# The first feed-forward reads a copy of x transposed by the host, loads its first operands in small pieces, and alternates between two output blocks

## The chip, the core and the metric

The kernel runs on one core of a Trainium2 chip. The metric is device time in microseconds, taken for the whole program; 2007.43 us is the median of three runs before the change (2007.25 to 2007.64). A difference of about 0.2%, or 4 us, is what a measurement of this kernel can tell from none.

The core has a matrix engine (PE, with its weight load shown as PEld), a vector engine (DVE), a scalar engine (ACT), GpSimd (POOL), and a queue engine (SP) that here issues nearly all transfers between device memory and the on-chip memory. Each engine works through its own list in order; they meet at semaphores.

## The reference

One layer of a hybrid encoder: x is 1024 tokens by 1024 features in float32. What matters here is the first step.

```python
def swiglu_ffn(x, w_gu, w_down):
    gu = x @ w_gu
    g, u = jnp.split(gu, 2, axis=-1)
    return (jax.nn.silu(g) * u) @ w_down

x = layer_norm(ALPHA * x + 0.5 * swiglu_ffn(x, ffn1_w_gu, ffn1_w_down), ln1_g, ln1_b)   # first feed-forward
x = layer_norm(ALPHA * x + hybrid_mixer(x, ...), ln2_g, ln2_b)                          # linear attention, top-k attention
x = layer_norm(ALPHA * x + 0.5 * swiglu_ffn(x, ffn2_w_gu, ffn2_w_down), ln3_g, ln3_b)   # second feed-forward
```

The hidden width is 2816, which is 22 blocks of 128: `w_gu` is 1024 by 5632, its left half for the gate and its right half for the up product. The output has the shape of x.

## The kernel before

**Precision.** Every matrix operand is held as two parts: `split` (L94 to L97) lets ACT round the float32 source to the matrix format (L96, the high part) and then lets DVE subtract that from the source (L97, the low part). A product of two operands is three matmuls: high by high (L336), high by low (L337), low by high (L338).

**Orientation.** The first product needs x with features on the partitions and tokens along the row, while x lies in memory by tokens. So blocks of 128 tokens are loaded by rows into the tiles `xin`, and `turn_in` (L278) has PE transpose four 128 by 128 pieces into a bank `tp` of the accumulator memory (L282), from where `split` makes the two parts. There are two `tp` banks.

**Seven products.** The feed-forwards cut x into four quarters, by feature half and token half. `sums["11"]`, `["21"]`, `["12"]`, `["22"]` are these quarters (first digit the feature half, second the token half), each four slices of 128 features by 512 tokens. From the second group of hidden blocks on, a recombination with seven products instead of eight is used, for which four more operands T1, T2, T3, T4 are formed from sums and differences of the quarters (L1245 to L1248, two on DVE and two on POOL for each of four blocks, in place in the `xin` tiles). Each of the eight operands is turned and split in four blocks: 32 calls of `turn_in` in this stage, 128 transposes.

**The first group.** `gate_up` (L388) computes the first two hidden blocks with the plain eight products. For token half c, for gate then up (i), two banks are taken, and for feature half k and hidden block f the call `product` adds four steps of three matmuls into bank f: 192 matmuls in all, each 128 by 128 by 512. The weights come from `quad_raw` (L292), 512 KB for a feature half, and `plain_weights` (L300) splits 128 by 1024 values at once. Then `quad` begins the second group with the products A11 by 11, A12 by 21, S4 by 22, S1 by T1, S2 by T2, S3 by T3, A22 by T4.

**The order of the work.** Loads are issued on SP's queue in program order: four pieces of x of 256 KB (features 0 to 511 of tokens 0 to 511), 512 KB of gate weights, four more pieces of x, 512 KB of gate weights, 1 MB of up weights, and the four 512 KB blocks of the second token half (L1336 to L1340). The body of the stage is under `in_order`, which chains the matrix engine's instructions in the order written: first the four turns of "11", then the products, with the other turns put between the steps by a list of due steps (`fills`, built by `spread`; `product` counts steps and runs what is due). What is outside a chain, and the order on all other engines, is decided at build time by a planner that simulates the program on a clock of its own and issues what it believes ready.

After the stage come ten more groups with seven products each, the down product of the feed-forward, the mixer, and the second feed-forward, whose front is the same code with `n` = 2 and operands that are made on chip.

## Time and profile before

| what | value |
|---|---|
| median of three runs | 2007.43 us (2007.25 to 2007.64) |
| profiled execution, first to last instruction (span) | 2003.4 us |
| what the median has above that span | 4.0 us |
| PE busy, share of the span | 1951.1 us, 97% |
| PE busy in the first 84 us | 74.8 us |
| DVE, ACT, POOL busy in the first 84 us | 45.1, 34.3, 27.0 us |
| transposes of the first feed-forward (L282), first 84 us | 128 |
| first matmul of a product begins | 11.07 us |

The page states no time of the profiled execution beside its span, so the span is set against the median of the runs. Times in the trace are microseconds from the first instruction; a row of the timeline gives start, duration, engine, line, operation, output and inputs, and in brackets how long the engine had been idle and what ended it. A row of the windows gives for a stretch the busy time of each engine with its number of instructions, then the granted clock of PE, the share of the transfer engines and GB/s. Matmuls overlap in the pipeline: the step from one start to the next tells more than a duration.

### The profile page before, as it was taken

Reading aid. Unit: us, or ns where it says so; the run is one execution under the profiler, and the core shown is the slowest. Engines: PE = TensorE matmul, PEld = TensorE weight load, DVE = VectorE, ACT = ScalarE, POOL = GpSimd, SP = SyncE. Lnnn points to the kernel's source line nnn. Section 1 sums busy time; section 2 is a strip of 40 time slices with the busy share of each in tenths; the row PEclk is TensorE's granted clock in tenths of the full one; section 3 lists DMA queues with packets and bytes.
Section 4 is the critical chain, followed back from the end, with each engine's and each line's share of the span. In section 5 each row is a group of like instructions: output and inputs, shape, how many; then the busy total and the mean of one; then the engine's idle time right before and its main releaser. Section 6 shows DMA issues by size and latency. Waiting matters only on the chain.

```text
span 2003.4 us, 26962 instructions
## 1 busy us (share of the span) xinstructions
PE 1951.1 (97%) x9752; PEld 1601.7 (80%) x9752; DVE 1478.2 (74%) x2330; ACT 824.8 (41%) x1321; POOL 590.6 (29%) x507
## 2 busy tenths in 40 slices
PE   8999999999999999998999899999999999999997
PEld 6888888888888788777777678788888888888886
DVE  5578778775658767999978567575777887866577
ACT  4332332334333444698643346333333232234331
POOL 3245445450001102143434100054444634510011
PEclk9999999999999999998999899999999999999999
DMA  5345444559665423011205651532444454487664
GB/s 178 111 148 179 158 147 163 174 195 312 204 203 195 131 64 110 28 53 39 79 22 163 172 135 38 177 118 83 147 155 147 168 168 139 166 285 262 198 197 150
DMA packets 193301, 298.43 MB, mean 149 GB/s; under 512 B 16384, under 2 KB 100496, under 8 KB 193168
## 3 DMA queue, kind: packets, MB, share of 16 engines
q1 hardware_dynamic: 189264, 291.48, 44.8%
q10 hardware_dynamic: 3264, 3.15, 0.5%
q0 software_dynamic: 640, 2.10, 0.3%
q8 instruction: 76, 1.25, 0.3%
q14 instruction: 57, 0.47, 0.1%
HBM read 205.96 MB, written 90.70 MB: 148 GB/s over the span
## 4 chain that ended last, share of the span: by engine, by line
PE 79%; DVE 10%; DMA 4%; ACT 3%; issue 2%; POOL 2%; SPq 0%; POOLq 0%; DVEq 0%; ACTq 0%
PE pd L508 18%; PE pq L338 13%; PE pq L337 13%; PE pq L336 13%; DVE junk L802 3%; PE pf L672 2%; PE pf L673 2%; PE pf L674 2%; PE pt L689 2%; PE pt L691 2%; PE pv L1158 2%; PE pt L690 2%; PE tpe L1142 2%; PE tp L282 1%; PE lg L1115 1%
## 5 line engine op out<-in xcount | busy, mean ns | idle before, releaser
L97 DVE TENSOR_TENSOR wloq<-rw,whiq 128x512 fp32r<-128x512 f32 (+1 forms) x208 | 214.7, 1035 | 111.1 <-ACT whiq L96 110.2
L97 DVE TENSOR_TENSOR wlod<-rd,whid 128x1024 fp32r<-128x1024 f32 x154 | 186.1, 1219 | 129.3 <-ACT whid L96 127.8
L96 ACT ACTIVATE whid<-rd 128x1024 fp32r<-128x1024 f32 x154 | 161.0, 1059 | 242.8 <-PE pd L508 174.2
L96 ACT ACTIVATE whiq<-rw 128x512 fp32r<-128x512 f32 (+1 forms) x208 | 163.5, 806 | 224.0 <-POOL rw L322 93.4
L508 PE MATMUL pd<-wlod,whid 128*128 128x512 f32 x616 | 239.8, 390 | 0.9 <-DVE wlod L97 0.8
L508 PE MATMUL pd<-whid,wlod 128*128 128x512 f32 x616 | 239.3, 389 | 0.0
L508 PE MATMUL pd<-whid 128*128 128x512 f32 x616 | 235.0, 391 | 0.0
L336 PE MATMUL pq<-b_h,whiq 128*128 128x512 f32 x576 | 229.1, 398 | 2.0 <-ACT b_h L96 2.0
L337 PE MATMUL pq<-b_l,whiq 128*128 128x512 f32 x576 | 225.5, 391 | 1.3 <-DVE b_l L97 1.3
L338 PE MATMUL pq<-b_h,wloq 128*128 128x512 f32 x576 | 225.3, 392 | 0.0
L224 POOL TENSOR_TENSOR rs<-ve,neghalf 128x1 f32<-128x1 f32 x24 | 33.8, 1410 | 539.1 <-DVE ve L242 539.1
L448 ACT ACTIVATE c<-c 128x512 f32<-128x512 f32 x80 | 50.4, 632 | 239.5 <-DVE c L372 147.6
L336 PE MATMUL pq<-xh,whiq 128*128 128x512 f32 x352 | 137.7, 391 | 0.0
L338 PE MATMUL pq<-xh,wloq 128*128 128x512 f32 x352 | 137.0, 389 | 0.0
L337 PE MATMUL pq<-xl,whiq 128*128 128x512 f32 x352 | 136.9, 389 | 0.0
L508 PEld LDWEIGHTS pd<-wlod,whid 128*128 128x128 f32 x616 | 115.6, 188 | 25.8 <-DVE wlod L97 2.1
L508 PEld LDWEIGHTS pd<-whid 128*128 128x128 f32 x616 | 115.5, 188 | 24.6 <-ACT whid L96 1.0
L508 PEld LDWEIGHTS pd<-whid,wlod 128*128 128x128 f32 x616 | 115.6, 188 | 24.0
L689 PE MATMUL pt<-whi,xh 128*128 128x512 f32 x320 | 130.0, 406 | 3.3 <-ACT stage L1490 1.6
L336 PEld LDWEIGHTS pq<-b_h,whiq 128*128 128x128 f32 x576 | 108.9, 189 | 23.9 <-ACT b_h L96 2.7
L337 PEld LDWEIGHTS pq<-b_l,whiq 128*128 128x128 f32 x576 | 108.9, 189 | 23.4 <-DVE b_l L97 2.1
L338 PEld LDWEIGHTS pq<-b_h,wloq 128*128 128x128 f32 x576 | 108.7, 189 | 23.1
(268 smaller groups left out, 4504.8 us busy)
## 6 DMA issues: line engine op xcount, KB each, us to landing
rw<-in_ffn_w_gu_dram SPq DMA_DIRECT2D x88, 512.0 KB, 4.2
rd<-h_dram SPq DMA_DIRECT2D x154, 256.0 KB, 3.5
h_dram<-c SPq DMA_DIRECT2D x148, 256.0 KB, 2.9
rt<-in_ffn_w_down_dram SPq DMA_DIRECT2D x44, 512.0 KB, 3.4
t_dram<-rt SPq DMA_DIRECT2D x44, 512.0 KB, 2.9
rd<-t_dram SPq DMA_DIRECT2D x88, 256.0 KB, 3.9
rd<-in_ffn_w_down_dram SPq DMA_DIRECT2D x66, 256.0 KB, 3.8
raw<-in_w_in_dram SPq DMA_DIRECT2D x20, 512.0 KB, 3.8
```

The source lines that it names most:

```text
L96: self.nc.scalar.activation(hi, src, AF.Copy)
L97: self.nc.vector.tensor_sub(lo, src, hi)
L336: mm(bank, wh[:, k, :], xh[:, k, :], start=(start and k == 0), stop=False)
L337: mm(bank, wh[:, k, :], xl[:, k, :], start=False, stop=False)
L338: mm(bank, wl[:, k, :], xh[:, k, :], start=False, stop=(stop and k == 3))
L448: nc.scalar.activation(t, t, AF.Silu)
L508: nc.tensor.matmul(bank, left, right, start=(i == 0 and n == 0), stop=(i == ng - 1 and n == 2))
L672: nc.tensor.matmul(pt[:m], wh[:, k, :m], xh[:, k, :], start=(k == 0), stop=False)
L673: nc.tensor.matmul(pt[:m], wh[:, k, :m], xl[:, k, :], start=False, stop=False)
L674: nc.tensor.matmul(pt[:m], wl[:, k, :m], xh[:, k, :], start=False, stop=(k == KD - 1))
L689: nc.tensor.matmul(pt, xh[:, k, cols], wh[:, k % 2, :], start=(k == 0), stop=False)
L802: V.tensor_scalar(junk[:, :n], scores[b], thr, None, ALU.is_ge, ALU.add, accum_out=cnt)
```

## The change

- The host hands the kernel a second input `xT`, x transposed (features by tokens); x itself is still an input, read later where the residual needs it. The `xin` tiles of the first feed-forward now hold, for block b = 4c + j and half h, features 128 (4h + j) onwards of token half c.
- Where the first feed-forward called `turn_in`, it now calls `split_in`: the two parts are made straight from the loaded tile, with no transpose and no `tp` bank. The second feed-forward keeps `turn_in`.
- The first half of the gate weights is loaded in four pieces of 128 KB, each behind a 256 KB piece of `xT`, and split in four pieces of 256 columns, alternating with the splits of "11".
- Then come one piece of "21", the second half of the gate weights in one load, the other three pieces of "21", the up weights, and eight pieces of the second token half.
- In the first group, the two banks take turns at every step of three matmuls instead of every four steps; `product` is cut into `step_of` for that.
- Eight matmuls of the identity with itself, whose result nobody reads, stand ahead of everything in PE's chain.

```diff
@@ -282,27 +282,42 @@
             self.nc.tensor.transpose(pt[:, k, :], src[:, k * P : (k + 1) * P], self.ident)
         self.w.split([t[:, :, j * P : (j + 1) * P] for t in self.sums[name]], pt)
+    def split_in(self, src, j, name):
+
+        self.w.split([t[:, j, :] for t in self.sums[name]], src)
+
...
-    def quad_raw(self, w_gu, c0, halves=(0, 1)):
+    def quad_raw(self, w_gu, c0, halves=(0, 1), between=None):
         r = []
         for k in halves:
             t = self.w.raw(self.uid("rw")).rearrange("p (k f) -> p k f", k=4)
+            r.append(t)
+            if between:
+                for j in range(4):
+                    f = k * 4 + j
+                    between(j)
+                    self.nc.sync.dma_start(t[:, j, :], w_gu[f * P : (f + 1) * P, c0 : c0 + 256])
+                continue
             self.nc.sync.dma_start(t, w_gu[k * 512 : (k + 1) * 512, c0 : c0 + 256].rearrange("(k p) f -> p k f", p=P))
-            r.append(t)
         return r
-    def plain_weights(self, r):
+    def plain_weights(self, r, between=None):
         out = {}
         for k, t in enumerate(r, 1):
             hl = [q.rearrange("p (k f) -> p k f", k=4) for q in self.w.pair(self.uid("q"))]
-            self.w.split(hl, t)
+            if between and k == 1:
+                for j in range(4):
+                    self.w.split([q[:, j, :] for q in hl], t[:, j, :])
+                    between(j)
+            else:
+                self.w.split(hl, t)
             for f in range(2):
                 out[f"A{f + 1}{k}"] = [q[:, :, f * P : (f + 1) * P] for q in hl]
         return out
@@ -329,16 +344,20 @@
     def product(self, bank, left, right, start=True, stop=True):
+        for k in range(4):
+            self.step_of(bank, left, right, k, start and k == 0, stop and k == 3)
+
+    def step_of(self, bank, left, right, k, start, stop):
+
         wh, wl = left
         xh, xl = self.sums[right]
         mm = self.nc.tensor.matmul
-        for k in range(4):
-            mm(bank, wh[:, k, :], xh[:, k, :], start=(start and k == 0), stop=False)
-            mm(bank, wh[:, k, :], xl[:, k, :], start=False, stop=False)
-            mm(bank, wl[:, k, :], xh[:, k, :], start=False, stop=(stop and k == 3))
-            self.step += 1
-            while self.fill and self.fill[0][0] <= self.step:
-                self.fill.pop(0)[1]()
+        mm(bank, wh[:, k, :], xh[:, k, :], start=start, stop=False)
+        mm(bank, wh[:, k, :], xl[:, k, :], start=False, stop=False)
+        mm(bank, wl[:, k, :], xh[:, k, :], start=False, stop=stop)
+        self.step += 1
+        while self.fill and self.fill[0][0] <= self.step:
+            self.fill.pop(0)[1]()
     def bank(self, ps):
         pool, tag, n = ((ps, "y", 2), (ps, "z", 2), (self.ps_pj, "pj", 2))[self.turn % 3]
@@ -424,8 +443,10 @@
             for i, a in enumerate(first):
                 banks = [self.bank(ps) for _ in range(2)]
                 for k in "12":
-                    for f in range(2):
-                        self.product(banks[f], a[f"A{f + 1}{k}"], k + c, start=(k == "1"), stop=(k == "2"))
+                    for j in range(4):
+                        for f in range(2):
+                            ends = [(k, j) == ("1", 0), (k, j) == ("2", 3)]
+                            self.step_of(banks[f], a[f"A{f + 1}{k}"], k + c, j, *ends)
                 for f in range(2):
                     if i == 0:
                         t = h[f, c] = self.c_tile(cp, "c")
@@ -1225,16 +1246,13 @@
         firsts, seconds = range(NB // 2), range(NB // 2, NB)
-        def front(n, first, blocks, held, left, ps, early, fed):
+        def front(n, first, t, held, left, ps, early, fed):
 
             V, G = nc.vector, nc.gpsimd
-
-            def t(b, half):
-                return blocks[b][:, half * 512 : half * 512 + 512]
             def turned(j, name):
                 src = {"T1": (j, 0), "T3": (j + 4, 0), "T2": (j + 4, 1), "T4": (j, 1)}
@@ -1250,7 +1268,10 @@
                         held.pop().close()
                         pool = left.enter_context(tc.tile_pool(name=f"t1_{n}", bufs=1, reuse_waits="tile"))
                         self.sums["T1"] = [pool.tile([P, 4, HT], F32R, name=f"t1{p}_{n}") for p in ("h", "l")]
-                    self.turn_in(t(*src[name]), j, name)
+                    if n == 1:
+                        self.split_in(t(*src[name]), j, name)
+                    else:
+                        self.turn_in(t(*src[name]), j, name)
                     if (j, name) == (3, "T4"):
                         held.pop().close()
                         cp.append((left.enter_context(tc.tile_pool(name=f"prod{n}", bufs=1, reuse_waits="tile")), 8))
@@ -1329,20 +1350,31 @@
                 self.two_sums(half_pair(xp, f"b{names[0]}_"), *names)
             held, xin = two_pools("xin")
             w_gu = a["ffn1_w_gu"][0]
-            raw = []
-            for c in range(2):
-                for b in firsts:
-                    cs = slice(c * 512, (c + 1) * 512)
-                    nc.sync.dma_start(xin[b][:, cs], x[0, b * P : (b + 1) * P, cs])
-                raw += self.quad_raw(w_gu, 0, (c,))
+
+            def t(b, half):
+                return xin[b][:, half * 512 : half * 512 + 512]
+
+            def load(c, j, half):
+                k = 4 * half + j
+                nc.sync.dma_start(t(4 * c + j, half), a["xT"][k * P : (k + 1) * P, c * 512 : (c + 1) * 512])
+
+            raw = self.quad_raw(w_gu, 0, (0,), lambda j: load(0, j, 0))
+            load(0, 0, 1)
+            raw += self.quad_raw(w_gu, 0, (1,))
+            for j in range(1, 4):
+                load(0, j, 1)
             raw = [raw, self.quad_raw(w_gu, FF)]
-            for b in seconds:
-                nc.sync.dma_start(xin[b], x[0, b * P : (b + 1) * P, :])
+            for half in range(2):
+                for j in range(4):
+                    load(1, j, half)
             with self.in_order():
-                for b in firsts:
-                    self.turn_in(xin[b][:, 0:512], b, "11")
-                first = [self.plain_weights(r) for r in raw]
-                work = front(1, first, xin, held, st, ps_ff, [(j, "21") for j in range(4)], ())
+                warm = self.ps_tp.tile([P, P], F32, tag="tp", name="warm")
+                for _ in range(8):
+                    nc.tensor.matmul(warm, self.ident, self.ident, start=True, stop=True)
+                self.split_in(t(0, 0), 0, "11")
+                first = [self.plain_weights(raw[0], lambda j: j < 3 and self.split_in(t(j + 1, 0), j + 1, "11"))]
+                first.append(self.plain_weights(raw[1]))
+                work = front(1, first, t, held, st, ps_ff, [(j, "21") for j in range(4)], ())
             for _ in work:
                 pass
         xp_stack = ExitStack()
@@ -1652,7 +1684,7 @@
             ln_stack.close()
             self.two_sums(self.new_half(0), "T2", "T3")
             first.append(self.plain_weights(raw[1]))
-            work = front(2, first, acc, held, st, ps_ff, (), (4, 5))
+            work = front(2, first, lambda b, half: acc[b][:, half * 512 : half * 512 + 512], held, st, ps_ff, (), (4, 5))
             ordered.close()
             for _ in work:
                 pass
@@ -1716,6 +1748,8 @@
         aps[name] = nc.dram_tensor(
             f"in_{name}_dram", arr.shape, mybir.dt.from_np(arr.dtype), kind="ExternalInput"
         ).ap()
+    arrays["in_xT_dram"] = np.ascontiguousarray(np.asarray(inputs["x"])[0].T)
+    aps["xT"] = nc.dram_tensor("in_xT_dram", (D, T), F32, kind="ExternalInput").ap()
     aps["out"] = nc.dram_tensor("out_0_dram", (1, T, D), F32, kind="ExternalOutput").ap()
     with tile.TileContext(nc, schedule_with_timeline_sim=True) as tc:
         emit(tc, aps)
```

## The prediction

> **What bounds the kernel now.** The first view is the page: the busy time of the engines and the chain of waits that ended last.
>
> ```profile
> span 2003.4 us, 26962 instructions
> PE 1951.1 (97%) x9752; PEld 1601.7 (80%) x9752; DVE 1478.2 (74%) x2330; ACT 824.8 (41%) x1321; POOL 590.6 (29%) x507
> ...
> PE 79%; DVE 10%; DMA 4%; ACT 3%; issue 2%; POOL 2%; SPq 0%; POOLq 0%; DVEq 0%; ACTq 0%
> ```
>
> PE bounds the program, but the shares are an average, and the change touches the first stage alone. So the second view is the windows: the stretch up to the last transpose of that stage, what follows it, and the mixer.
>
> ```profile
> 0.00:84.00 84.00, 74.80 (x368) 60.50 (x369) 45.06 (x69) 34.34 (x52) 27.03 (x29) 1.00 0.43 147
> ...
> 72.00:200.00 128.00, 128.00 (x574) 105.98 (x573) 96.28 (x107) 38.97 (x60) 60.25 (x40) 1.00 0.46 156
> 200.00:400.00 200.00, 200.00 (x884) 165.61 (x883) 157.29 (x171) 64.45 (x98) 91.58 (x60) 1.00 0.48 161
> 400.00:600.00 200.00, 199.94 (x881) 165.00 (x880) 129.35 (x141) 76.12 (x83) 26.42 (x22) 1.00 0.70 227
> ...
> 800.00:1000.00 200.00, 190.21 (x1008) 152.25 (x1006) 189.76 (x564) 159.35 (x296) 71.43 (x86) 0.97 0.18 51
> 1000.00:1200.00 200.00, 186.23 (x1274) 148.21 (x1274) 134.29 (x323) 86.23 (x209) 48.73 (x58) 0.97 0.46 122
> 1200.00:1400.00 200.00, 194.43 (x1295) 161.09 (x1295) 131.84 (x228) 85.76 (x136) 50.86 (x32) 0.99 0.30 101
> ```
>
> From 72 to 600 us PE is never free for want of data (527.94 of 528 us), and DVE has a fifth to spare. So what PE is spared before 84 us is handed on whole: everything behind starts earlier by that much. Idle PE time, 9.2 us, lies in the first 84 us. The third view is the timeline of the start.
>
> ```profile
> 0.74 1.81 SPq L1336 DMA_DIRECT2D xin<-in_x_dram  x4
> 3.91 1.94 PE L282 MATMUL tp<-ident,xin 128*128 128x128 f32 x8 [3.91 <-DMA xin<-in_x_dram]
> 5.07 1.28 ACT L96 ACT_TABLE_LOAD   x1 [5.07 <-PE tp L282]
> ...
> 8.99 1.06 ACT L96 ACTIVATE whiq<-rw 128x1024 fp32r<-128x1024 f32 x1 [1.54 <-DMA rw<-in_ffn_w_gu_dram]
> ...
> 11.07 0.80 PE L336 MATMUL pq<-b_h,whiq 128*128 128x512 f32 x1 [1.36 <-ACT b_h L96]
> ...
> 12.56 0.79 PE L337 MATMUL pq<-b_l,whiq 128*128 128x512 f32 x1 [0.69 <-DVE b_l L97]
> 13.15 0.63 PE L338 MATMUL pq<-b_h,wloq 128*128 128x512 f32 x1
> 13.57 0.63 PE L336 MATMUL pq<-b_h,whiq 128*128 128x512 f32 x1
> 13.71 1.06 ACT L96 ACTIVATE whiq<-rw 128x1024 fp32r<-128x1024 f32 x1 [2.69 <-DMA rw<-in_ffn_w_gu_dram]
> ...
> 15.21 1.06 ACT L96 ACTIVATE whiq<-rw 128x1024 fp32r<-128x1024 f32 x1 [0.45 <-DMA rw<-in_ffn_w_gu_dram]
> 16.37 0.40 PE L338 MATMUL pq<-b_h,wloq 128*128 128x512 f32 x1
> ...
> 23.52 0.50 PE L337 MATMUL pq<-b_l,whiq 128*128 128x512 f32 x1 [0.56 <-DVE b_l L97]
> ```
>
> The first x piece lands at 3.9 us, two blocks are turned, ACT loads its table, the weights land at 8.99 as one 512 KB load, and the first product starts at 11.07. Matmuls then start 0.42 us apart (13.15 to 13.57) and from about 16 us at the full pace. PE last waits at 23.52. The fourth view is the end of the stage on PE.
>
> ```profile
> 83.11 0.39 PE L338 MATMUL pq<-b_h,wloq 128*128 128x512 f32 x1
> 83.34 0.60 PE L282 MATMUL tp<-ident,xin 128*128 128x128 f32 x4
> 83.69 0.48 PE L338 MATMUL pq<-t1h,wloq 128*128 128x512 f32 x1
> 84.01 0.40 PE L336 MATMUL pq<-bT_h,whiq 128*128 128x512 f32 x1
> ...
> 89.27 0.39 PE L338 MATMUL pq<-bT_h,wloq 128*128 128x512 f32 x1
> ```
>
> The full pace is 0.2287 us: 23 steps from 84.01 to 89.27. Four transposes cost 84.01 - 83.11 - 2 x 0.2287 = 0.44 us. At 83.69 the last turn is over.
>
> ```profile
> L282 PE MATMUL tp<-ident,xin 128*128 128x128 f32 x128 | 21.2, 296 | 5.9 <-DMA xin<-in_x_dram 3.9 <-DVE b_l L97 1.9
> ...
> L96 ACT ACTIVATE whiq<-rw 128x1024 fp32r<-128x1024 f32 x8 | 8.5, 1058 | 8.6 <-DMA rw<-in_ffn_w_gu_dram 4.7 <-PE pq L337 3.9
> L96 ACT ACTIVATE whiq<-rw 128x512 fp32r<-128x512 f32 x9 | 5.4, 627 | 10.3 <-PE pq L337 4.8 <-issue 3.7 <-DMA rw<-in_ffn_w_gu_dram 1.8
> L1247 DVE TENSOR_TENSOR xin<-xin,xin 128x512 f32<-128x512 f32 x4 | 4.5, 1136 | 5.0 <-POOL xin L1246 5.0
> ```
>
> Of the 368 PE instructions up to 84 us, 128 are transposes and 240 are matmuls of products, one of them begun at 83.69. So 239 matmuls stood before that point, 239 x 0.2287 = 54.7 us at full pace; the other 29.0 us are the late start, the slow pace, waits, and transposes (24 turns at full pace alone are 24 x 0.44 = 10.6 us).
>
> **The change part by part.** I rebuild the time at which those 239 matmuls are done.
>
> *Start.* The first piece of `xT` has the size of the first piece of x and the same place in the queue, so it lands at 3.9. ACT's table load, which waited for PE's transpose, now waits for the load: 5.2. The high part of 128 by 512 from on-chip memory takes 0.63 (the row above with 512 columns): 5.8. A weight piece of 256 columns is not in the trace; from 0.63 at 512 and 1.06 at 1024 columns it is an estimated 0.41: 6.2, with a hand-over of 0.2 the first matmul starts at 6.4. Bounds: 5.1, if the table is loaded before the data; 10.0, if the pieces land no sooner than the 512 KB did (8.99 plus the two ACT steps).
>
> *Arrival.* The four pairs are 1.5 MB, as many bytes as stood in the queue up to and with the first weights, which landed at 8.99. So the fourth pair lands at about 9.0 and those between at 5.6 and 7.3; the second half of the gate weights (2.25 MB) at about 11.4, between 8.99 and 13.71; all of "21" (3.0 MB) at 13.7, and the up weights as before, from 15.2. PE comes to the fourth slice at 6.4 + 18 x 0.2287 + 1.9 (next item) = 12.4, the split of it is ready two splits of ACT and two of DVE behind 9.0, about 11. To the second half it comes at 13.8, and that is split on ACT (1.06) and DVE (about as long) by 13.7. The up weights are wanted at 19.3 and split by 17.5. So two blocks in turn, with six matmuls for each slice, just hide the loads. With eight loads at 0.45 us each (four took 1.81) SP has issued the four pairs by 4.4, ahead of their landing; 23 issues in place of 16 delay only the next weights, which wait for buffers anyway.
>
> *Slow pace.* In the trace the pace doubles some 3.4 us after PE works without gaps (12.56 to about 16). The granted clock is 1.00 in the row to 84 us, so that column doesn't show it; the starts do. Eight identity matmuls, at the pace of the eight transposes (1.94 us), end near 4, and a gap to 6.4 follows. I take it that they change nothing: from 6.4 to about 10.4 some 10 matmuls at 0.42, each 0.19 too long, cost 1.9 us. Bounds 0 (they suffice) and 3.6 (a stretch twice as long). The Trainium skill, "TensorE: Matmul & The Clock Gate", Part 1, says that the clock is released after about 3.4 us of sustained work, watched in free-running windows. This agrees with the 3.4 us here and gives the same sum; by the full effect of a warm-up it would be 1.9 us less.
>
> *Transposes.* All 128 go from PE: nothing replaces them there, and 54.7 us of matmuls stay. 6.4 + 1.9 + 54.7 = 63.0, against 83.7: 20.7 us earlier. The eight waste matmuls lie in time in which PE has no data.
>
> *Splits.* ACT gains 0.03 us a piece, no matter at 34 of 84 us. DVE's subtraction now has both inputs in on-chip memory, where it had one in the accumulators. What that costs is in this view of the same stage, DVE and POOL rows by time.
>
> ```profile
> 28.00 1.30 POOL L319 TENSOR_TENSOR rw<-rw,rw 128x512 f32<-128x512 f32 x1 [1.23 <-DVE wloq L97]
> 28.45 1.40 DVE L1247 TENSOR_TENSOR xin<-xin,xin 128x512 f32<-128x512 f32 x1
> 29.77 1.33 DVE L97 TENSOR_TENSOR b_l<-tp,b_h 128x512 fp32r<-128x512 f32 x2
> 29.93 1.30 POOL L1248 TENSOR_TENSOR xin<-xin,xin 128x512 f32<-128x512 f32 x1 [0.63 <-DVE xin L1247]
> ...
> 33.67 1.30 POOL L321 TENSOR_TENSOR rw<-rw,rw 128x512 f32<-128x512 f32 x1
> 33.76 1.76 DVE L1247 TENSOR_TENSOR xin<-xin,xin 128x512 f32<-128x512 f32 x1 [2.65 <-POOL xin L1246]
> ...
> 39.41 0.69 DVE L1247 TENSOR_TENSOR xin<-xin,xin 128x512 f32<-128x512 f32 x1 [1.15 <-POOL xin L1246]
> ```
>
> L1247, both inputs in on-chip memory, takes 0.69 us alone and 1.40 or 1.76 beside a POOL operation; the split from `tp` at 29.77 ran two in 1.33 beside one, undisturbed. So up to 32 subtractions (28 ahead of S1 by T1) now can be held up. The Trainium skill, "SBUF — State Buffer", Who interferes with whom, has it as a rule: a DVE instruction with two inputs in SBUF contends with GpSimd reads, one with a single such input doesn't. This trace agrees, and the rule speaks against this change.
>
> The price: POOL works 27.0 us in the stretch to 84 us. If every us of it held DVE up, less the 1.8 that the four L1247 already lose (4 x (1.136 - 0.69)), DVE would need 45.1 + 25.2 = 70.3 us, and has 63.0 - 6.4 = 56.6 us from PE's start to the same point: 13.7 us of stall at worst. With half of it, 57.7 us, DVE just about keeps pace. I take 2 us, nearer the lower end since POOL works in a third of the stretch only, and since three products stand ahead of the first that needs a T operand; bounds 0 and 13.7. If DVE falls behind there, the low part of T1 is late next, and PE waits for it.
>
> *Alternating banks* changes neither number nor shape of matmuls. Both blocks now end three matmuls apart, so two evictions of 0.6 to 0.7 us come together; six banks take turns, and the next product has its own. Nothing; at worst one eviction, 0.7 us, at the four ends.
>
> *Sum.* 20.7 - 2 = 18.7 us. Span 2003.4 - 18.7 = 1984.7; with the 4.0 us by which the median of the runs stands above the span, 1988.7, so **1989 us**. From the bounds: 20.7 + 1.9 + 1.3 = 23.9 earlier at best (1983.5); 20.7 - 3.6 + 1.9 - 13.7 = 5.3 at worst with a timely start (2002.1); that both worst cases meet I leave out of the range.
>
> **The rivals.**
>
> *The pieces land together.* If transfers in flight share the bandwidth, the first pair is complete only when the fourth is. For it: the first x piece landed when 512 KB had been issued behind it. Against: it did land at 3.9, 5 us ahead of the weights. The start is then 10.0, 3.6 us later, and the time 1992.
>
> *DVE becomes the bound of the stage.* Three quarters of the worst stall, 10 us, 8 more than I took: 1997. For it: 1.40 and 1.76 against 0.69. Against: POOL is busy for a third of the stretch only. The rule of the Trainium skill on "SBUF — State Buffer", Who interferes with whom, is the ground for it.
>
> *The transposes were hidden.* If the loads or the splits set the pace throughout, removing PE work brings the start alone, 4.7 us: 2002.7. Against it stands PE without a gap from 24 us on.
>
> *Slower: the planner orders the mixer anew.* The order there comes from a simulated clock, and the start moves on it. From 800 to 1400 us PE idles 9.8 + 13.8 + 5.6 = 29.1 us, with DVE at 95% in the first third, so an order that delays DVE is paid at once. Were that idle time doubled, the program would lose 29.1 - 18.7 = 10.4 us: 2018. It decides from 18.7 us of new idle time. Against it: a start that is earlier by a constant leaves the order of what comes later as it is.
>
> **How the numbers follow.** The forecast has 0.60 (with its own range 1985 to 1993), pieces together 0.13, DVE 0.15, transposes hidden 0.04, the planner's order 0.08, half of it slower and half a part of the gain lost. From 1983 to 1999 it holds the first three, less the tails of the forecast: eight in ten. Faster by over 0.2% (4 us, about what a measurement of this kernel can tell) is all but 0.04 for no change and 0.04 for slower: 0.92.
>
> **What would show it.** No L282 row before 84 us; the first L336 with `b_h` near 6.4; a pace of 0.42 to about 10; PE without a wait from there; T2's first product (84.01 now) near 65; L97 on `b_l` above 0.68 mean, with rows near 1.3 beside POOL; the same PE idle time from 780 to 1380. I am wrong if PE waits for DVE for several us between 25 and 65, if the first product starts past 9, or if the idle time of the mixer moves by more than 5 us.

## The result, and the profile after

The median of four runs of the changed kernel is 1989.86 us (1987.2 to 1991.97), that of four runs of the kernel before 2007.54 us (2007.25 to 2007.8). The ratio is 0.9913, with a 95% interval of 0.9902 to 0.9925: 17.7 us faster, where 18.7 us was forecast. The profiled execution of the changed kernel took 1987.2 us, 1.8 more than its span. These are the busy times and the chain of its page.

```profile
span 1985.4 us, 26743 instructions
PE 1933.6 (97%) x9640; PEld 1589.3 (80%) x9640; DVE 1486.2 (75%) x2333; ACT 824.3 (42%) x1324; POOL 598.8 (30%) x507
...
PE 71%; DVE 12%; DMA 6%; POOL 4%; issue 3%; ACT 3%; SPq 0%; POOLq 0%; DVEq 0%; ACTq 0%
```

PE has 17.5 us less to do (128 transposes, 21.2 us, less 3.8 for the identity matmuls) and still bounds the program, but its part of the chain fell from 79% to 71%, and POOL has doubled its own to 4%. The timeline shows the start, on PE and ACT, and the place where the first product of T2 begins.

```profile
0.73 1.28 ACT L96 ACT_TABLE_LOAD   x1 [0.73 <-PEq L1743]
1.74 3.78 PE L1373 MATMUL warm<-ident 128*128 128x128 f32 x16 [1.74 <-POOL ident masks.py:199]
4.05 0.42 ACT L96 ACTIVATE whiq<-rw 128x256 fp32r<-128x256 f32 x1 [2.03 <-DMA rw<-in_ffn_w_gu_dram]
5.17 0.76 PE L355 MATMUL pq<-b_h,whiq 128*128 128x512 f32 x1
...
6.10 0.39 PE L357 MATMUL pq<-b_h,wloq 128*128 128x512 f32 x1
6.33 0.40 PE L355 MATMUL pq<-b_h,whiq 128*128 128x512 f32 x1
...
12.48 0.50 PE L355 MATMUL pq<-b_h,whiq 128*128 128x512 f32 x1 [0.97 <-ACT whiq L96]
13.74 0.50 PE L357 MATMUL pq<-b_h,wloq 128*128 128x512 f32 x1 [0.53 <-DVE wloq L97]
...
62.16 0.39 PE L357 MATMUL pq<-t1h,wloq 128*128 128x512 f32 x1
62.38 0.39 PE L355 MATMUL pq<-bT_h,whiq 128*128 128x512 f32 x1
```

No transpose stands ahead of 62.38, and the first product of T2 starts there, 21.6 us ahead of the 84.01 before. PE starts its products at 5.17 and is at the full pace from 6.10 (the next start is 0.23 later). It waits twice, 1.5 us in all, for the second half of the gate weights. Its second wait is for DVE's low part of these weights; otherwise it does not wait for DVE on the way. The next rows, of POOL, ACT, DVE and PE, show where it does.

```profile
68.28 1.30 POOL L337 TENSOR_TENSOR rw<-rw,rw 128x512 f32<-128x512 f32 x1
69.61 1.06 ACT L96 ACTIVATE whiq<-rw 128x1024 fp32r<-128x1024 f32 x1 [2.67 <-POOL rw L337]
70.70 1.23 DVE L97 TENSOR_TENSOR wloq<-rw,whiq 128x1024 fp32r<-128x1024 f32 x1 [4.43 <-ACT whiq L96]
76.81 0.68 DVE L404 TENSOR_TENSOR c<-c,pq 128x512 f32<-128x512 f32 x1
77.54 0.50 PE L355 MATMUL pq<-b_h,whiq 128*128 128x512 f32 x1 [1.40 <-DVE c L404]
```

POOL ends its sums of the gate weights (L334 to L337) at 69.6, four of some 1.5 us in a row. ACT and DVE, which had waited 2.67 and 4.43 us, split them, and the additions of products queued behind these splits on DVE, up to L404, end at 77.5. PE needs the bank that L404 empties and loses 1.40 us. The groups of instructions up to 84 us show one reason why POOL is late; the fence behind it has a row of the same view of the kernel before.

```profile
L97 DVE TENSOR_TENSOR b_l<-xin,b_h 128x512 fp32r<-128x512 f32 x20 | 16.4, 850 | 1.9 <-ACT b_h L96 1.8
L97 DVE TENSOR_TENSOR bT_l<-xin,bT_h 128x512 fp32r<-128x512 f32 x8 | 10.7, 1364 | 0.0
...
L1266 POOL TENSOR_TENSOR xin<-xin,xin 128x512 f32<-128x512 f32 x4 | 6.7, 1672 | 5.5 <-DVE xin L1265 5.5
```

```profile
L1248 POOL TENSOR_TENSOR xin<-xin,xin 128x512 f32<-128x512 f32 x4 | 5.2, 1295 | 2.9 <-DVE xin L1247 2.9
```

DVE's subtraction with two inputs in on-chip memory takes 0.85 and 1.36 us in the mean, against 0.69 undisturbed; POOL's operation takes 1.67 in place of 1.30. Both engines pay. Behind this stage some of the gain is given back. The windows of after from the first down matmul, from the first of the mixer and from the first score product on, and those of before at the same points:

```profile
434.00:650.10 216.10, 214.16 (x958) 176.46 (x957) 146.81 (x175) 84.87 (x89) 9.26 (x5) 1.00 0.69 224
650.10:1089.60 439.50, 421.74 (x2274) 344.35 (x2273) 363.75 (x872) 262.48 (x499) 138.07 (x190) 0.98 0.24 73
1089.60:1985.40 895.80, 868.30 (x4525) 713.72 (x4523) 630.78 (x902) 325.86 (x507) 246.88 (x165) 0.99 0.50 161
```

```profile
454.00:668.80 214.80, 213.99 (x957) 176.32 (x956) 146.05 (x174) 84.96 (x89) 9.26 (x5) 1.00 0.70 225
668.80:1106.90 438.10, 421.91 (x2273) 343.28 (x2272) 365.12 (x872) 262.30 (x499) 134.98 (x190) 0.98 0.24 73
1106.90:2003.40 896.50, 870.37 (x4525) 715.29 (x4523) 629.77 (x902) 326.39 (x507) 246.21 (x165) 0.99 0.50 161
```

Of the 20.0 us that are left at the first down matmul (454.0 to 434.0), 1.3 go in the down product (216.1 us for 214.8) and 1.4 in the mixer (439.5 for 438.1); 0.7 come back after it (895.8 for 896.5). What the down product lost shows in its own rows, of ACT and PE, and in the row of SP at which the loads behind those of x (L1314, before L1293) are issued; first after, then before.

```profile
449.49 0.33 SPq L228 DMA_DIRECT2D g_bc<-in_ln_g_dram  x1
...
461.37 1.06 ACT L96 ACTIVATE whid<-rd 128x1024 fp32r<-128x1024 f32 x1 [15.23 <-DMA rd<-h_dram]
462.48 1.20 PE L529 MATMUL pd<-whid 128*128 128x512 f32 x4 [1.12 <-ACT whid L96]
```

```profile
468.36 0.33 SPq L228 DMA_DIRECT2D g_bc<-in_ln_g_dram  x1
...
481.22 0.97 PE L508 MATMUL pd<-whid 128*128 128x512 f32 x3
```

PE waits 1.12 us for a piece of h that is still being loaded; before it did not wait there (its row has no bracket). PE came 20.0 us earlier, but SP issued the load of L228, which stands ahead of the next pieces, only 18.9 us earlier: 15.5 us behind the first down matmul, where it was 14.4.

### The profile page after: what moved, and what is told of

Same layout as the page of the kernel before. It is cut to its first block, busy times and chain, and to the rows that moved or that the text cites. A ratio compares the mean times of both kernels' runs of the same rounds, so it can differ in the third digit from the quotient of the medians.

```text
span 1985.4 us, 26743 instructions
## 1 busy us (share of the span) xinstructions
PE 1933.6 (97%) x9640; PEld 1589.3 (80%) x9640; DVE 1486.2 (75%) x2333; ACT 824.3 (42%) x1324; POOL 598.8 (30%) x507
## 3 DMA queue, kind: packets, MB, share of 16 engines
q8 instruction: 76, 1.25, 0.3%
## 4 chain that ended last, share of the span: by engine, by line
PE 71%; DVE 12%; DMA 6%; POOL 4%; issue 3%; ACT 3%; SPq 0%; POOLq 0%; DVEq 0%; ACTq 0%
PE pd L529 18%; PE pq L355 10%; PE pq L356 10%; PE pq L357 10%; DVE junk L823 3%; PE pf L693 3%; PE pf L694 3%; PE pf L695 3%; PE pt L710 2%; PE pv L1179 2%; PE pt L712 2%; PE pt L711 2%; PE tpe L1163 2%; DMA t_dram<-rt 1%; DMA rd<-in_ffn_w_down_dram 1%
## 5 line engine op out<-in xcount | busy, mean ns | idle before, releaser
L97 DVE TENSOR_TENSOR wloq<-rw,whiq 128x512 fp32r<-128x512 f32 (+2 forms) x211 | 212.7, 1010 | 122.5 <-ACT whiq L96 121.3
L96 ACT ACTIVATE whiq<-rw 128x512 fp32r<-128x512 f32 (+2 forms) x211 | 164.2, 797 | 213.2 <-POOL rw L337 105.6
```

Of the source, the lines that this page charges most:

```text
L96: self.nc.scalar.activation(hi, src, AF.Copy)
L97: self.nc.vector.tensor_sub(lo, src, hi)
```

## Experiments

The theory: the gain is the removed transposes (some 16 us) and a start some 5 us earlier through the small pieces, handed on whole until PE waits for something that did not come earlier by as much. The rivals: the start alone makes the gain, because loads or splits set the pace; the identity matmuls or the alternation carry a part; what is lost behind 77 us is not POOL's lateness but the spread from run to run. The kernels below ran on three chips, the kernel before on each of them, so ratios are compared, and times on one chip. Line numbers are those of the changed kernel; in the two kernels named pieces2 they are one higher.

**The changed kernel again (after_again).** Nothing is edited.

> The changed kernel once more, to see where its runs differ (1987.2 to 1992.0 us, while the kernel before stayed within 0.6 us). Theory A, the spread arises at the start, where the matrix engine's pace may or may not have doubled by the first product: then a slower execution shows first matmuls 0.42 us apart and S2 by T2 begins later than 62.4 us, by up to 1.6 us. Theory B, the spread arises in the mixer, where the granted clock dips to 0.97: then S2 by T2 begins at 62.4 us again in every profile, and what differs lies behind 640 us. Time: 1990 us, within 2.5 us.

Measured: 1992.3 us, ratio 0.9929 (0.9916 to 0.9941). The first 84 us repeat: full pace from the start, T2's first product at 63.0, waits of 1.6 and 0.5 us for the second half of the weights and of 1.5 for L404. The down product waits 1.9 us in place of 1.1. With the third measurement below, the gain in the medians is 17.7, 13.5 and 14.5 us, and single traces differ behind 430 us.

**Without the identity matmuls (no_warm).**

```diff
-                warm = self.ps_tp.tile([P, P], F32, tag="tp", name="warm")
-                for _ in range(8):
-                    nc.tensor.matmul(warm, self.ident, self.ident, start=True, stop=True)
```

> The eight identity matmuls are left out, all else as in the changed kernel. Theory A, they double the pace before the first product: without them the first 8 matmuls from 5.2 us start 0.42 us apart, 1.6 us in all, and the stage ends 1.6 us later (S2 by T2 at 64.0, 1991.5 us). Theory B, the slow pace is hidden behind the second half of the gate weights, for which PE waits anyway (1.0 us to 12.48 and 0.5 us to 13.74): then the slow pace is seen, but S2 by T2 comes at most 0.5 us later and the time stays within noise. As the prediction took it, the eight are without effect: then the pace at 5.2 us is the full one here too.

Measured: 1993.05 us, ratio 0.9939 (0.9927 to 0.9952), not told apart from the changed kernel. Its timeline on PE:

```profile
5.07 0.79 PE L355 MATMUL pq<-b_h,whiq 128*128 128x512 f32 x1 [5.07 <-ACT b_h L96]
...
10.23 0.56 PE L357 MATMUL pq<-b_h,wloq 128*128 128x512 f32 x1
10.63 0.40 PE L355 MATMUL pq<-b_h,whiq 128*128 128x512 f32 x1
...
80.22 0.79 PE L355 MATMUL pq<-b_h,whiq 128*128 128x512 f32 x1 [3.33 <-DVE c L404]
```

Products start some 0.4 us apart until 10.63, so the identity matmuls do what the prediction denied them: they bring the full pace forward, in three traces by 3 to 5 us. It is worth next to nothing here. With half the pace PE comes later to the second half of the gate weights and waits for it 0.3 us in place of 2.1; T2's first product stands at 63.0 in both traces. The longer wait for L404 (3.33 against 1.5) was seen in one trace of this kernel, whose execution was the slowest of its five (1998.19 us), and whether the edit causes it stays open. With it the first down matmul comes at 439.2, 4.5 us later than in after_again; PE then does not wait for h in the down product, and 2.5 us of the 4.5 are left at the first mixer matmul (654.1 against 651.6).

**The old order of blocks (no_turns).**

```diff
-                    for j in range(4):
-                        for f in range(2):
-                            ends = [(k, j) == ("1", 0), (k, j) == ("2", 3)]
-                            self.step_of(banks[f], a[f"A{f + 1}{k}"], k + c, j, *ends)
+                    for f in range(2):
+                        self.product(banks[f], a[f"A{f + 1}{k}"], k + c, start=(k == "1"), stop=(k == "2"))
```

> The two output blocks one after the other, four steps each, as before the change; loads in pieces, xT and identity matmuls stay. Theory A: alternation hides the arrival of the slices; without it PE needs the fourth slice after 9 matmuls, at 7.3 us, while it is split near 9.9, so PE waits some 2.5 us there. Of this 1.5 us are won back, since PE comes later to the second half of the weights and need not wait for it: net 0.5 to 1 us. Theory B: taking banks in turn has a price or a gain of its own on PE; then the step between matmuls (0.2287 us) changes and the time moves by more than 2 us.

Measured: 1992.65 us, ratio 0.993 (0.9917 to 0.9944); T2's first product at 62.8. PE waits 0.3 us more at 8.05 and less later. Two blocks in turn are worth nothing that can be measured, with the pieces landing as they do.

**The old loads (big_loads).** The pieces of `xT` and the gate weights are loaded in the order and size of before, and split whole; the rest of the change stays.

```diff
-            raw = self.quad_raw(w_gu, 0, (0,), lambda j: load(0, j, 0))
...
+            for half in range(2):
+                for j in range(4):
+                    load(0, j, half)
+                raw += self.quad_raw(w_gu, 0, (half,))
...
-                self.split_in(t(0, 0), 0, "11")
-                first = [self.plain_weights(raw[0], lambda j: j < 3 and self.split_in(t(j + 1, 0), j + 1, "11"))]
-                first.append(self.plain_weights(raw[1]))
+                for j in range(4):
+                    self.split_in(t(j, 0), j, "11")
+                first = [self.plain_weights(r) for r in raw]
```

> xT, alternation and identity matmuls stay; the loads go back to their old order and size: four pieces of xT, 512 KB of gate weights as one load split at once, four pieces, 512 KB. Theory A: the start sets the time, so the first product begins near 10 us and its low weights come near 11.3, and the stage ends 4 to 4.5 us later (S2 by T2 near 66.5, about 1994 us). Theory B: DVE, busy 8 of every 8 us from 16 to 64 us, paces the stage or POOL paces what follows (PE waits 1.4 us at 77.5): then most of the late start is given back by 100 us and the loss is 1 to 3 us.

Measured: 1996.35 us, ratio 0.9952 (0.9939 to 0.9964), 4.05 us above after_again beside it. From its view of the waits on PE up to 445 us:

```profile
PE pq L355 <- ACT whiq L96: 5.5, 1, 5.5
```

The first product starts at 11.04 and T2's at 68.0, 5.0 us later than in after_again. The wait for L404 is gone, since POOL has those 5 us more; the first down matmul is only 3.2 us later. So the pieces bring 5 us at the start, and about a third of it is paid back at L404.

**The transposed copy alone (xT_only).** Old loads, old order of blocks, no identity matmuls: the three edits above together. Of the change, only `xT` in place of the transposes is left, with its second token half still in eight pieces.

> The kernel before with the transposed copy alone: no transposes, but the old order and size of the loads, the blocks one after the other, and no identity matmuls. Theory A, the transposes were PE work on the path that sets the end: 24 turns at full pace are worth 10.6 us and the first eight, at the slow pace, up to 4 us more; the first product begins near 10.1 to 11 us, at the slow pace for 3.4 us, and S2 by T2 near 67 to 69 us (84.0 before), so about 1994 to 1997 us. Theory B, the transposes were hidden behind the loads and the splits: then S2 by T2 comes no sooner than 79 us and the time is above 2001 us.

Measured: 1996.45 us against 2006.55 of the kernel before on that chip, ratio 0.9951 (0.9937 to 0.9964).

```profile
10.32 0.79 PE L355 MATMUL pq<-b_h,whiq 128*128 128x512 f32 x1 [10.32 <-ACT whiq L96]
```

The start has moved by 0.7 us (11.07 to 10.32), and T2's first product is at 67.48, 16.9 us ahead of before_again's 84.35. The transposes were on the path: the rival by which they were hidden falls. In time 10.1 us of these 16.9 are left; in the two profiled traces the lead is still 16.9 us at the first down matmul and 11.8 at the end.

**POOL's sums of x on DVE (dve_sums).** In the first feed-forward the sums of L1264 and L1266 go to DVE; so POOL has less to do and DVE is disturbed less.

```diff
-                        G.tensor_sub(t(j + 4, 0), t(j + 4, 1), t(j + 4, 0))
+                        (V if n == 1 else G).tensor_sub(t(j + 4, 0), t(j + 4, 1), t(j + 4, 0))
...
-                        G.tensor_sub(t(j, 1), t(j, 1), t(j + 4, 1))
+                        (V if n == 1 else G).tensor_sub(t(j, 1), t(j, 1), t(j + 4, 1))
```

> The changed kernel with the eight sums that POOL made for T2 and T4 (13.4 us on POOL there) put on DVE. Theory A, the two engines hold each other up: DVE gets 8 times 0.68 us more, and loses what POOL cost it (b_l 0.85, bT_l 1.36, the two other sums 0.96 and 1.23 us mean, all 0.68 to 0.69 alone: about 12 us), so DVE is less busy to 64 us (57.6 us now, near 51), POOL's weight sums start sooner and PE's wait of 1.4 to 1.5 us for the combined product (L404) goes; about 1.5 us less up to the first down product (434.0 to 434.8 us now). Theory B, DVE's work is what fills these 48 us: then DVE stays busy throughout, T1 comes later, and PE waits for DVE before 64 us.

Measured: 1989.41 us, ratio 0.9919 (0.9904 to 0.9934). The groups up to 84 us, and POOL's last sum of the first weights with DVE's L404 in its timeline:

```profile
L97 DVE TENSOR_TENSOR b_l<-xin,b_h 128x512 fp32r<-128x512 f32 x20 | 13.2, 690 | 2.6 <-ACT b_h L96 2.5
L97 DVE TENSOR_TENSOR bT_l<-xin,bT_h 128x512 fp32r<-128x512 f32 x8 | 7.1, 890 | 0.0
```

```profile
63.98 1.29 POOL L337 TENSOR_TENSOR rw<-rw,rw 128x512 f32<-128x512 f32 x1
...
72.51 0.68 DVE L404 TENSOR_TENSOR c<-c,pq 128x512 f32<-128x512 f32 x1
```

DVE did eight operations more and was busy for less: 55.84 us up to 64 us in place of 57.55. The splits fell from 850 to 690 ns and from 1364 to 890. POOL's sum comes 4.3 us earlier (68.28 to 63.98), L404 too (76.81 to 72.51), and PE's wait for it is gone. That the wait is gone proves little by itself, since PE is later here too (T2's first product at 64.7). But in all eleven traces of kernels with `xT`, L404 begins 8.51 to 8.54 us behind the start of POOL's last sum, wherever PE stands, and in pieces2_dve below, where PE is earlier than in any other (T2's first product at 60.4), L404 begins at 72.05 and PE does not wait. That shows POOL's lateness as the cause of the wait. How much of the lateness comes from longer operations and how much from POOL's own work is not shown, since the edit takes the eight operations off POOL altogether. In this trace a new loss of about that size stands at 13 to 19 us (below), so that the first down matmul gains nothing (434.7).

**The second half of the gate weights in pieces (pieces2), and with the sums on DVE (pieces2_dve, pieces2_dve_b).** The load of the second half is cut into four, each behind its piece of "21", and split in four pieces, as those of the first are; the other two kernels, which are equal, have the edit of dve_sums too.

```diff
-            if between and k == 1:
+            if between:
...
-                    between(j)
+                    if k == 1:
+                        between(j)
...
-            load(0, 0, 1)
-            raw += self.quad_raw(w_gu, 0, (1,))
-            for j in range(1, 4):
-                load(0, j, 1)
+            raw += self.quad_raw(w_gu, 0, (1,), lambda j: load(0, j, 1))
```

> The changed kernel with the second half of the gate weights in four pieces, POOL's sums left on POOL. Theory A: the waits for that half go (1.5 us) and with them the slow window that may follow, so S2 by T2 begins near 61 us; but POOL and DVE still hold each other up, so PE's wait for the combined product (L404) stays and grows by what was won, to about 3 us: the first down product near 434 us, no gain in the time. Theory B: the wait at L404 has nothing to do with POOL's sums: then it goes here too and the first down product comes near 431 us.

> As dve_sums, and the second half of the gate weights too is loaded and split in four pieces, each behind its piece of 21. Theory A: PE's waits for that half (1.0 to 1.6 us for the high part, 0.5 us for the low part) go too, so S2 by T2 begins near 61 us and the first down product near 431.5 us; about 3 us less than the changed kernel. Theory B: the pieces are three issues more and smaller loads, so they land later or ACT's order holds the fifth slice up: then PE still waits 1 us or more between 11 and 14 us.

> The kernel with pieces in the second half and the sums on DVE once more, beside the changed kernel on one chip. Theory A: 3.5 to 4.5 us less up to the first down product (430.3 against 434.0 to 434.8 us), all of which reaches the end: about 4 us less than after_third in the median. Theory B: the mixer takes it back, since its order and the dips of the clock there move: less than 2 us.

Measured: pieces2 1993.16 us, ratio 0.9931 (0.9919 to 0.9943); pieces2_dve 1988.39, ratio 0.9911 (0.9897 to 0.9925); pieces2_dve_b 1986.77, ratio 0.99 (0.9887 to 0.9913). From the waits on PE up to 445 us of pieces2, then of pieces2_dve_b:

```profile
PE pq L356 <- DVE c L405: 3.3, 1, 3.3
...
PE pq L358 <- DVE wloq L97: 0.3, 1, 0.3
```

```profile
PE pq L356 <- ACT whiq L96: 0.4, 1, 0.4
```

The pieces alone take the wait for the weights from 1.5 to 0.3 us and bring T2 to 61.3, and it all goes again in the wait for `c`, 3.3 us. With the sums on DVE that wait is gone, and the first down matmul comes at 430.3 and 431.5. Neither edit by itself brings PE there sooner than the 434.0 to 436.6 of the changed kernel; together they bring 2.5 to 6.3 us. pieces2_dve_b ran 6.1 us below the changed kernel beside it (1992.89); the intervals of the two ratios overlap from 0.9911 to 0.9913. It is the fastest version found. From chip to chip the gain in time is less clear: the ratio of pieces2_dve, 0.9911, is that of the changed kernel's first measurement, 0.9913.

**Again, both kernels (before_again, after_third, before_third).** Nothing is edited.

> The kernel before once more, for a second trace of it. If the spread of the runs comes from where the granted clock dips in the mixer (Theory B of the first look), this trace agrees with the first one to 0.3 us up to the first matmul of the mixer (668.8 us) and may differ by up to 4 us behind it, at the first score product (1106.9 us). If it comes from the start (Theory A), S2 by T2 begins elsewhere than at 84.0 us. Time 2004 to 2008 us.

> The changed kernel a third time, on the same chip as the next three. Theory A: to the first down product it is within 1 us of 434.0 and 434.8 us, unless the wait for the second half of the gate weights near 12 to 14 us lets the clock fall back (seen once in dve_sums, 15.5 to 18.9 us at 0.42 us a matmul), which costs 1.6 us more. Behind 650 us the mixer takes 439 to 443 us to its first score product. Theory B, the mixer's length is the chip's: then it is the same in after_third and before_third of this call. Time 1987 to 1993 us.

> The kernel before a third time, for a third trace: from the first mixer matmul (668.6 to 668.8 us) to the first score product 438.1 and 440.6 us so far, against 439.5 and 443.1 us in the two traces of the changed kernel. Theory A, the planner's new order of the mixer costs about 2 us: 438 to 441 us here, 440 us or more in after_third. Theory B, both draw from one spread: the two overlap fully.

Measured: before_again 2006.67 us, ratio 1.0 (0.9991 to 1.0009); before_third 2007.49, ratio 0.9999 (0.9989 to 1.0009); after_third 1992.89, ratio 0.9925 (0.9911 to 0.994). The traces give the lead of after over before at each point, in us, the second pair from two chips:

| point | after and before | after_again and before_again | after_third and before_third |
|---|---|---|---|
| first product of T2 | 21.6 | 21.4 | 21.2 |
| first down matmul | 20.0 | 19.5 | 17.0 |
| first mixer matmul | 18.7 | 17.0 | 11.7 |
| first score product | 17.3 | 14.5 | 8.8 |
| last down matmul | 18.0 | 14.1 | 9.3 |

The lead at T2 repeats within 0.5 us. What is given back behind it differs, from 3.7 to 11.9 us in single traces. The PE timeline of after_third has its two largest pieces:

```profile
78.56 0.50 PE L355 MATMUL pq<-b_h,whiq 128*128 128x512 f32 x1 [2.28 <-DVE c L404]
...
79.16 0.63 PE L357 MATMUL pq<-b_h,wloq 128*128 128x512 f32 x1
79.58 0.63 PE L355 MATMUL pq<-b_h,whiq 128*128 128x512 f32 x1
...
82.54 0.39 PE L356 MATMUL pq<-b_l,whiq 128*128 128x512 f32 x1
...
467.59 1.58 PE L529 MATMUL pd<-whid 128*128 128x512 f32 x4 [3.61 <-ACT whid L96]
```

The wait at L404 is 2.28 us here, the one in the down product 3.61, and behind the first the pace is 0.42 us until 82.5, which costs some 1.6 us more (8 steps by 0.2). The wait in the down product goes with SP: where L228 is issued 14.0 to 14.4 us behind the first down matmul (before, before_third) there is none; at 15.5 (after) it is 1.1, at 16.1 to 16.6 (no_turns, after_again, after_third) 1.9 to 3.6. The other traces fit in: none at 13.6 and 14.3 (before_again, no_warm), 0.4 to 1.3 us from 14.8 to 15.8 (pieces2_dve, xT_only, dve_sums), 1.8 to 2.2 from 16.4 to 16.7 (big_loads, pieces2_dve_b, pieces2). Why SP comes to its loads later, measured from PE, was not tried.

## Why the prediction was right, and which steps were not

*The matmul term and the transposes held.* 239 matmuls at 0.2287 us are 54.7; from 5.17 that is 59.8, with the two waits of 1.5 us 61.3, and the 240th stands at 62.16, the rest being slower steps at the start and right behind each wait. xT_only shows the transposes on the path: 16.9 us by themselves.

*The number is in part luck.* The forecast had 18.7 us at T2 and all of it at the end. Measured were 21.6 us at T2, since the start and the pace were better than said, and 18.0 at the end of the trace (17.7 in the median), since 3.7 were given back on the way. The two errors nearly cancel here; in the two later measurements, with 13.5 and 14.5 us in the median, they cancel less.

*Start: 5.17 in place of 6.4.* The table load did not wait for the data. It stood at 0.73, which was the case of the stated lower bound; in big_loads and xT_only it did wait for the first piece of `xT` (3.71 and 3.67), as the forecast took it. The pieces landed one after the other: the high part of the first weights is begun at 4.05.

*Slow pace: mis-sized, 0.5 in place of 1.9.* Only the first two steps are slow, 0.59 and 0.34 us; in after_third the first five are, and cost 1.2. The identity matmuls took 3.78 us, not 1.94: 16 rows for 8 instructions, so that PE worked without a gap until the products began. "I take it that they change nothing" was wrong of the pace (no_warm: half of it until 10.63) and right of the time, for another reason: what the pace gains is waited out at the second half of the weights.

*Arrival: the step "that is split on ACT (1.06) and DVE by 13.7" held, "just hide the loads" did not.* PE came to these weights at 11.5 rather than 13.8, since it started earlier and at full pace, and waited 1.5 us. Start and pace, 1.2 and 1.4 us better than said, paid for this.

*Splits: near in size, wrong in place.* From the windows of after:

```profile
0.00:64.00 64.00, 60.77 (x264) 49.71 (x265) 57.55 (x76) 33.07 (x54) 27.92 (x26) 1.00 0.49 165
```

DVE was busy for 57.55 us up to 64, and the forecast had 57.7 if half of POOL's time held it up. That they agree so closely is chance: 5.2 us of the 57.55 are L430 to L432, work that stood behind 84 us in the kernel before. And the low part of T1 was not late for it, as the prediction had it: PE waits for none of DVE's splits of x. The prediction let only DVE pay; POOL paid too (1.30 to 1.67 us), its weight sums came late for the earlier PE, and the price fell due at L404, 1.4 us (1.5 and 2.28 in the others) for the 2 us taken. The Trainium skill, "SBUF — State Buffer", Who interferes with whom, says that the order of issue decides which of the two is blocked; that both are longer here is in keeping with it, but no row shows which was issued first.

*"Handed on whole" was wrong from 434 us on.* From 72 to 600 us PE had no gap, so the forecast let everything move along. The loads in the down product did not move by as much, and PE waits there now. The mixer takes longer too (next item).

*Alternating banks: nothing, as said.* T2's first product is at 62.8 without the turns (no_turns) and at 63.0 with them (after_again).

*The planner's order* was a rival with 0.08 and is not what happened on its scale: PE's idle time from 780 to 1380 us is 31.7 us, against 29.1 from 800 to 1400 before. The argument against it was wrong all the same. The order in the mixer did change: between the first mixer matmul and the first score product 76 of DVE's 871 instructions and 8 of PE's 2272 stand elsewhere in the sequence, alike in all three traces of after. This stretch takes 439.5, 443.1 and 440.8 us there, 441.0 to 443.3 in the eight traces of the edited kernels, and 438.1, 440.6 and 438.1 before: 442.2 in the mean of eleven against 438.9 in the mean of three. So some 3 us go there. On the two chips with a trace of both, the kernel before is the shorter by 0.4 to 4.6 us. That the order is the cause is not shown, since no run has the old order behind the new start.

*The 4.0 us from span to median came out at 4.5* (1989.86 - 1985.4), but not as the constant that the sum made of it. The profiled execution itself takes 1.8 us more than its span (2.4 in before_third); the rest is that it was the quickest of its four. With the traces of after_again or after_third the span would be 1990.5 or 1994.2.

*Pieces together, DVE as the bound, transposes hidden:* the first and the last fall by the start at 5.17 and by xT_only, the second by PE's row of waits, which in the first trace of the changed kernel has nothing of DVE ahead of 77 us but the 0.53 us for the weights.

## What to carry to other kernels

Work that is taken off the engine that bounds a stage is worth its time at the full pace only up to the next thing that does not come earlier with it; after forecasting the gain, go along the path and ask of each load and each helper engine by how much it moves. Where two engines contend, cost both of them, and look for the price at the later one's next consumer; two small faults that hide one another (weights late, `c` late) have to be mended together. One profiled execution places the cause, but a difference of a few microseconds far behind the edit needs several.

## What the runs showed of the hardware

Short waits can cost twice. After the start and up to 660 us the traces have six waits of PE of 2.17 us or more (2.17 and 3.33 in pieces2, 2.28 and 3.61 in after_third, 2.60 in no_turns, 3.33 in no_warm), and behind each of them six to twelve steps from matmul to matmul take some 0.43 us in place of 0.23. Behind none of the nine single waits from 0.90 to 2.06 us is it so. Two short ones close together did it once, in dve_sums, here in its timeline on PE:

```profile
14.46 0.50 PE L357 MATMUL pq<-b_h,wloq 128*128 128x512 f32 x1 [0.53 <-DVE wloq L97]
15.51 0.63 PE L355 MATMUL pq<-b_h,whiq 128*128 128x512 f32 x1
15.93 0.63 PE L356 MATMUL pq<-b_l,whiq 128*128 128x512 f32 x1
...
18.92 0.40 PE L357 MATMUL pq<-b_h,wloq 128*128 128x512 f32 x1
```

That wait had one of 1.25 us before it, at 13.20. The length of the two does not decide it: 0.97 and 0.53 us at the same place in after, and even 1.65 and 0.53 in after_again, had no such effect. What else does was not tried. The Trainium skill, "TensorE: Matmul & The Clock Gate", Why this matters for your kernels, warns of idle gaps of PE over about 3 us; here 2.17 us was enough.
